# Memory's inputs in places of their own, both heads' sample scores in one bank, and three early products in a fused transformer step

## The chip, the core and the metric

The kernel runs on one core of a Trainium2 chip. The metric is the device time of one execution in microseconds (us). Before the change it is 1798.29 us, the median of three runs (1796.28 to 1800.38).

## The reference

One inference step of a streaming encoder layer, for a prompt of 1024 frames and a sample of 64 frames that share the weights; model width 1024, 16 heads of 64 (8 of kind A, 8 of kind B). All in float32.

```python
def mem_kv(mem, g_mem, w_mkv, g_mk):                 # mem (1, 256, 1024): the memory
    kv = rms_norm(mem, g_mem) @ w_mkv                # (256, 2048)
    k = rms_norm(kv[..., :D_MODEL].reshape(b, n, H_M, HEAD_DIM_M), g_mk)
    v = kv[..., D_MODEL:].reshape(b, n, H_M, HEAD_DIM_M)
    return k, v
...
# prompt: qa .. vb, logf = in_proj(rms_norm(xp), w_in, ...)
oa = chunk_band_attn_prompt(qa, ka, va, rel_bias)    # A: band of 8 chunks of 64
ob = forget_attn_prompt(qb, kb, vb, logf)            # B: causal, with a forget gate
xp = xp + concat([oa, ob]) @ w_o
xp = xp + mem_attend(rms_norm(xp), mk, mv, w_mq, g_mq, w_mo)
xp = xp + conv_ffn(rms_norm(xp), ...)
# sample: the same, with keys and values from caches (A: 512 rows, B: 1024 rows) ahead of its own 64
oa = chunk_band_attn_sample(qa, ka, va, cache_a_k, cache_a_v, rel_bias)
ob = forget_attn_sample(qb, kb, vb, logf, cache_b_k, cache_b_v, cache_b_logf)
xs = xs + concat([oa, ob]) @ w_o
```

## The kernel before

Every matmul of float32 data is made of three on TensorE (PE): a tensor is split into a rounded high part (a cast on ScalarE, ACT) and a low part (a subtraction on VectorE, DVE, or GpSimd, POOL), and high times high, low times high and high times low are added up in PSUM. The kernel is one long program in stages: input projection and prompt attention of eight pairs of heads; the tail of the last pair's attention; memory's keys and values; the sample's attention; the output projection w_o; memory attention; the feed-forward. A scheduler sets each engine's order from the order in which the code gives the work out, except for instructions in `tc.keep_in_program_order`. `weave(main, subs)` lays matmul pieces (`main`) between smaller jobs (`subs`).

The change lies between the tail of attention and the first products of w_o, 574 to 734 us of the span.

*Memory.* `load_mem` brings memory's frames (memT) in two halves into tiles `s` of the attention's own pool `wk`, and splits them with the gain into `mhi` and `mlo` (`gained`: ACT L256, DVE L257). `load_wm` brings the weights w_mkv in 16 loads of 512 KB into `mwraw`, two buffers; `split_wm` casts half a load to `mwhi` (ACT, L657) and subtracts `mwlo` (L658), by turns on POOL and DVE. `mem_piece` makes six matmuls (L668); four pieces make one of 16 units (column block n, half t of the 256 rows), 64 pieces and 384 matmuls in all. `mem_end` evicts a unit: for keys the norm's inverse root by `rsq` (two steps on ACT, three on DVE), for values a scaled copy. `mem_turn` transposes keys a unit later.

*Attention's tail.* The last pair's scores, sums and evictions come in four calls of `substeps()`. `otmp` (ACT, L552) and `mix` (DVE, L553) evict the attention's sum out of PSUM bank O; mix goes to DRAM (`mixd`). `LEFT` says how many memory pieces are woven into each of the four calls: 0, 0, 0, 15.

*Samples.* A `Sample` is a pair of heads of the 64 sample frames; the list has four of kind B first (1024 cached rows), then four of kind A (512). `prep` transposes q and k and splits them, and adds the gate on POOL (L750); `splitk` splits the cached keys of one head into `kchi` (ACT, L762) and `kclo` (DVE, L763); `splitv` the values into `vc` (ACT, L770; POOL, L771). `score(h)` makes one head's scores (L783; L784 for the sample's own 64 rows) with the q of both heads as weights, so that only 64 of the 128 rows of bank S are of use; a reduction on DVE adds the bias and finds the maximum (L786, L788) for those 64 rows. After the second head: the exponential on ACT (L796), the reciprocal, and the normalization on POOL (L798). `turn` transposes the probabilities (L810) and splits them into `pth` and `ptl` (L811, L812), `sum` multiplies by the values (L823) and adds up both parts in `st` (L830) and `su` (L831), `out` transposes into `smix` (L835, L837). In turn x of the loop, sample x is scored, sample x-1 is finished and sample x+1 prepared, with `PER[x]` memory pieces woven in: 4, 8, 9, 12, 6, 5, 6, 0, 0.

*Products.* When no memory piece is left, `open_left` closes memory's pool and opens in its place the weight stream (`raw`, `hi`, `lo`: L904, L905), the tiles `a` of the attention's result and their stage; `load_mix` and `split_mix` bring `mixd` in eight loads and split it (ACT L964, DVE L965), all eight in one turn of the loop (`MIXES`). A product is 24 matmuls of 384 columns (L922). Two products are made early, beside sample 7's end and behind it; `project` makes the rest in the order ORDER, and evicts each into x1d, the residual sum.

The split of memory's weights, and the pool that holds them:

```python
left = ExitStack()
mp = left.enter_context(tc.tile_pool(name="mp", bufs=1, side="left"))
...
def split_wm(n, y):
    raw = wraw[n, y // 2][:, 2 * (y % 2):2 * (y % 2) + 2]
    ...
    act.copy(hi, raw)
    (dve if y % 2 else pool).tensor_tensor(lo, raw, f32(hi), op=ALU.subtract)
```

Of the kernel before, what the change touches and what calls it, by code (L numbers as in the profile page):

```python
# [26 lines left out]
LEFT = (0, 0, 0, 15)  # L27
PER = (4, 8, 9, 12, 6, 5, 6, 0, 0)
STAGE, MIXES = 4, 8
# [12 lines left out]
def hybrid_step(ctx: ExitStack, tc: tile.TileContext, i: dict, o: dict):  # L42
# [590 lines left out]

    left = ExitStack()
    mp = left.enter_context(tc.tile_pool(name="mp", bufs=1, side="left"))
    kmd = dram.tile([4, 2, P, 256], F32, name="kmd")
    vmd = dram.tile([2, P, T], F32, name="vmd")
    mem = [mp.tile([P, KT, 256], F32R, name=f"m{n}") for n in ("hi", "lo")]
# [3 lines left out]
    def load_mem(z):  # L642
        raw = wk.tile([P, N], F32, name="s", bufs=4)[:, :1024].rearrange("p (k t) -> p k t", k=4)
        nc.sync.dma_start(raw, i["memT"][4 * z:4 * z + 4].rearrange("k p t -> p k t"))
        for k in range(4):
            gained(mem[0][:, 4 * z + k], mem[1][:, 4 * z + k], raw[:, k], gcol[:, 3, 4 * z + k:4 * z + k + 1])

    def load_wm(n, z):
        raw = mp.tile([P, 4, 256], F32, name="mwraw", bufs=2)
        nc.sync.dma_start(raw.rearrange("p k c -> p (k c)"), i["w_mkv"][n, z])  # L650
        wraw[n, z] = raw

    def split_wm(n, y):
# [3 lines left out]
        act.copy(hi, raw)  # L657
        (dve if y % 2 else pool).tensor_tensor(lo, raw, f32(hi), op=ALU.subtract)  # L658
# [15 lines left out]
    def mem_end(n, t):  # L674
        pj = mpj.pop((n, t))[:, :256]
        kv = mp.tile([P, 256], F32, name="kv", bufs=2)
# [3 lines left out]
        if n < 4:  # L680
# [4 lines left out]
            dve.tensor_scalar(ms, ms, emem[:, t:t + 1], None, op0=ALU.add)  # L685
            rsq(mp, ms, r, 1)
# [17 lines left out]
    class Sample:  # L704
# [31 lines left out]
        def prep(self):  # L736
# [7 lines left out]
            self.q = mq.tile([P, 2, S], F32R, name="sq_", bufs=2)  # L744
            self.kn = [mq.tile([P, 2, S], F32R, name=f"skn{x}", bufs=2) for x in range(2)]
            gained(self.q, self.q[64:], tq[:, 0:2, :S], gd[:, p // 4, 0:1], slice(64, P))
# [9 lines left out]
        def splitk(self, h):  # L756
            k = self.kraw.pop(0)
            for c in range(self.nc):
# [3 lines left out]
                act.copy(hi, raw)  # L762
                dve.tensor_tensor(lo, raw, f32(hi), op=ALU.subtract)  # L763
                self.kc[h, c] = hi, lo

        def splitv(self):
            for c in range(self.nc):
                raw = self.craw.pop(0)
                v = mq.tile([P, 4, 2, 2, 64], F32R, name="vc", bufs=3)
                act.copy(v[:, :, :, 0], raw)  # L770
                pool.tensor_tensor(v[:, :, :, 1], raw, f32(v[:, :, :, 0]), op=ALU.subtract)  # L771
                self.vc.append(v)

        def score(self, h):
            n = self.ctx
            b, q, r = self.s, self.q.rearrange("p h t -> p (h t)"), slice(h * S, h * S + S)
            if h == 0:
                self.mx = wk.tile([P, 2], F32, name="smx", bufs=2)
            sp = ps.tile([P, 2, 512], F32, name="S", bufs=1)
            sn = bank("tq").rearrange("p (a b) -> p a b", a=4)  # L780
            for m in range(2):
                for c in range(self.nc):
                    pe.matmul(sp[:, c], q, self.kc[h, c][m], start=m == 0, stop=m == 1)  # L783
                pe.matmul(sn[:, 0, :S], q, self.kn[m][:, h], start=m == 0, stop=m == 1)  # L784
            sf = sp.rearrange("p a b -> p (a b)")
            dve.tensor_tensor_reduce(out=b[r, :n], in0=sf[r, :n], in1=b[r, :n], scale=-1.0, scalar=BIG,  # L786
                                     op0=ALU.add, op1=ALU.min, accum_out=self.mx[r, 0:1])
            dve.tensor_tensor_reduce(out=b[r, n:n + S], in0=sn[r, 0, :S], in1=b[r, n:n + S], scale=-1.0, scalar=BIG,  # L788
                                     op0=ALU.add, op1=ALU.min, accum_out=self.mx[r, 1:2])
            if h == 0:  # L790
                return
# [3 lines left out]
            dve.tensor_tensor(m1, self.mx[:, 0:1], self.mx[:, 1:2], op=ALU.min)  # L795
            act.activation(b[:, :n], b[:, :n], ACT.Exp, bias=m1, scale=-1.0, accum_out=sm)  # L796
            dve.reciprocal(sm, sm)
# [72 lines left out]
    for n in LEFT:  # L870
        step(n, substeps())
# [978 lines left out]
```

## Time and profile before

| | |
|---|---|
| time, median of 3 runs | 1798.29 us (1796.28 to 1800.38) |
| the profiled execution's own time | 1797.27 us |
| its span, first to last instruction | 1795.2 us |
| mean granted clock of TensorE | 0.990 |
| busy share PE, DVE, ACT, POOL | 96%, 68%, 52%, 37% |
| memory's matmuls, first to last | 602.2 to 704.4 us |

The profile covers one execution. A timeline row gives the start, the duration, the engine, the line, the operation, output<-input, the shapes, how many rows are drawn together, and in brackets the idle time of the engine ahead of it with the event that ended it. PE overlaps its matmuls, so the distance of two starts says what one costs, and the duration does not. A group's row gives the count, then busy us and the mean ns of one, then the idle time of the engine ahead of the group and what ended it. The clock column is the share of full speed that TensorE was granted.

### The profile page before, as it was taken

How to read it: one execution, taken by the hardware profiler on the slowest of the kernel's cores; microseconds unless marked ns; L12 is line 12 of the kernel's file. 1: busy time of each engine (PE TensorE's matmuls, PEld its weight loads, DVE VectorE, ACT ScalarE, POOL GpSimd, SP SyncE). 2: the span in 40 equal slices, each digit the busy share in tenths (PEclk: the TensorE clock that was granted, in tenths of full speed). 3: DMA queues.
4: the chain of work that ended last, by engine and by line, in shares of the span. 5: the costliest groups of instructions: out<-in, count | busy, mean ns of one | idle time of the engine just before them, and what ended most of it. 6: DMA issues, size and time to landing. Idle time of an engine off the chain costs nothing. (4 is left out here: it accounts for less than half of the span.)

```text
span 1795.2 us, 34082 instructions
## 1 busy us (share of the span) xinstructions
PE 1716.4 (96%) x12432; PEld 1664.3 (93%) x12432; DVE 1224.5 (68%) x2710; ACT 930.2 (52%) x2042; POOL 664.1 (37%) x1025
## 2 busy tenths in 40 slices
PE   6898999999998888999999999999999999999999
PEld 5788999999997777999999999999999999999999
DVE  5778667677677797433444379877777777677994
ACT  5656667677677577433555455433333333434332
POOL 5656657779777554443444521100000000000000
PEclk8999999999999999999999999999999999999999
DMA  7322222122112776542111563222222222794232
GB/s 244 93 68 57 62 75 72 55 72 76 47 59 79 221 246 216 164 137 65 54 54 60 149 216 103 78 79 74 87 83 89 73 73 72 254 312 157 77 118 80
DMA packets 134248, 199.87 MB, mean 111 GB/s; under 512 B 20968, under 2 KB 74088, under 8 KB 134080
## 3 DMA queue, kind: packets, MB, share of 16 engines
q1 hardware_dynamic: 134080, 197.70, 34.8%
q8 instruction: 98, 1.61, 0.4%
q14 instruction: 70, 0.57, 0.1%
HBM read 155.35 MB, written 45.44 MB: 112 GB/s over the span
## 5 line engine op out<-in xcount | busy, mean ns | idle before, releaser
L288 PE MATMUL pj<-whi,xhi 128*128 128x384 f32 (+1 forms) x512 | 194.9, 381 | 3.4 <-ACT xhi L130 1.7
L288 PE MATMUL pj<-wlo,xhi 128*128 128x384 f32 (+1 forms) x512 | 176.1, 344 | 3.4 <-POOL wlo L123 3.4
L288 PE MATMUL pj<-whi,xlo 128*128 128x384 f32 (+1 forms) x512 | 174.7, 341 | 0.7 <-DVE xlo L131 0.7
L1540 POOL COPY s<-gp 128x2 f32<-128x2 f32 x22 | 15.8, 719 | 335.8 <-DVE gp L1539 335.8
L1434 PE MATMUL W<-h,hi 128*128 128x272 f32 x704 | 134.4, 288 | 1.4 <-ACT qlo L1570 1.4
L493 ACT ACTIVATE s<-s,mx 128x640 f32<-128x640 f32 (+7 forms) x128 | 94.4, 737 | 75.0 <-DVE mx L491 74.1
L1731 PE MATMUL W<-f,hi 128*128 128x272 f32 x672 | 127.7, 288 | 3.5 <-DVE f L1299 1.7
L530 DVE TENSOR_TENSOR ptl<-PT,pth 128x512 fp32r<-128x512 f32 (+2 forms) x192 | 99.5, 522 | 39.1 <-ACT pth L529 37.0
L1434 PEld LDWEIGHTS W<-h,hi 128*128 128x128 f32 x704 | 110.8, 188 | 1.7 <-ACT qlo L1570 1.6
L1731 PEld LDWEIGHTS W<-f,hi 128*128 128x128 f32 x672 | 105.3, 188 | 4.4 <-DVE gp L1505 2.4
L243 POOL TENSOR_TENSOR r<-m,mhalf 128x4 f32<-128x4 f32 (+1 forms) x72 | 73.9, 1027 | 92.4 <-DVE m L242 90.0
L529 ACT CAST pth<-PT 128x512 fp32r<-128x512 f32 (+2 forms) x192 | 85.0, 448 | 39.5 <-PE PT L528 37.9
L288 PEld LDWEIGHTS pj<-whi,xhi 128*128 128x128 f32 x512 | 98.9, 193 | 5.2 <-ACT xhi L130 2.3
L288 PEld LDWEIGHTS pj<-wlo,xhi 128*128 128x128 f32 x512 | 98.7, 193 | 5.3 <-POOL wlo L123 5.1
L1434 PE MATMUL W<-h,lo 128*128 128x272 f32 x352 | 101.8, 289 | 0.0
L1298 ACT CAST hi<-raw 128x512 fp32r<-128x512 f32 x68 | 42.2, 621 | 109.1 <-PE W L1434 59.1
L288 PEld LDWEIGHTS pj<-whi,xlo 128*128 128x128 f32 x512 | 97.3, 190 | 1.4 <-DVE xlo L131 1.2
L1731 PE MATMUL W<-f,lo 128*128 128x272 f32 x336 | 96.7, 288 | 0.0
L528 PE MATMUL PT<-ident,s 128*128 128x128 f32 x528 | 89.7, 277 | 6.2 <-DVE ptl L530 5.4
L246 POOL TENSOR_SCALAR qk<-qkraw,r 128x128 f32<-128x128 f32 x256 | 91.5, 375 | 5.9
L488 PE MATMUL S<-kh,q 128*128 128x256 f32 (+1 forms) x304 | 77.4, 280 | 12.8 <-DVE mx L491 12.7
L922 PE MATMUL pj<-a,hi 128*128 128x384 f32 (+1 forms) x352 | 89.5, 337 | 0.0
(606 smaller groups left out, 6051.3 us busy)
## 6 DMA issues: line engine op xcount, KB each, us to landing
raw<-in_w_down_dram SPq DMA_DIRECT2D x45, 256.0 KB, 2.9
wraw<-in_w_dram SPq DMA_DIRECT2D x56, 192.0 KB, 2.4
raw<-in_w_up_dram SPq DMA_DIRECT2D x41, 256.0 KB, 2.8
h<-ad SPq DMA_DIRECT2D x32, 272.0 KB, 4.7
mwraw<-in_w_mkv_dram SPq DMA_DIRECT2D x16, 512.0 KB, 5.2
raw<-in_w_mo_dram SPq DMA_DIRECT2D x32, 256.0 KB, 3.3
kvraw<-in_w_down_dram SPq DMA_DIRECT2D x32, 256.0 KB, 3.3
ad<-t SPq DMA_DIRECT2D x22, 272.0 KB, 2.1
```

The source lines that it names most:

```text
L243: pool.tensor_tensor(r[:rows], m[:rows], mhalf[:rows, 0:4], op=ALU.pow)
L246: pool.tensor_scalar(qk[:rows, h], raw[:rows, h * 64:(h + 1) * 64].rearrange("p (o d) -> p o d", o=1).broadcast_to([rows, 2, 64]), r[:rows ...
L288: pe.matmul(pj[:, :nw], x2[a][:, k, t * P:(t + 1) * P], wt[k][b][:, :nw], start=n == 0, stop=n == 3 * KT - 1)
L488: pe.matmul(sp[:, a:a + (k1 - k0) * P], q, kk[:, h, src], start=m == 0, stop=m == 1)
L493: act.activation(s[:, :n], s[:, :n], ACT.Exp, bias=mx, scale=-1.0, accum_out=sm)
L528: pe.transpose(pt[:, b - ch[0]], self.s[j][:, (b - w0) * P:(b - w0 + 1) * P], ident)
L529: act.copy(hi[:, f:f + n, j], pt[:, f:f + n])
L530: dve.tensor_tensor(lo[:, f:f + n, j], pt[:, f:f + n], f32(hi[:, f:f + n, j]), op=ALU.subtract)
L922: pe.matmul(out()[:, :cn], w[a][:, k % 4], x[b][k][:, c0:c0 + cn], start=k == 0 and n == 0, stop=k == KT - 1 and n == 2)
L1298: act.copy(hi, t)
L1434: pe.matmul(w[:, z, :Q], a(p, j), rights[j][b][:, z * Q:z * Q + Q], start=fresh and begin and j == 0 and x == 0, stop=final and end and j ...
L1731: pe.matmul(ws[m][:, z, :Q], la[p][:, m * P:(m + 1) * P], ra[b][:, z * Q:z * Q + Q], start=first and y == 0 and what in opening, stop=fina ...
```

## The change

1. *Memory's inputs.* memT gets tiles of its own (`mwraw`, now four buffers) and is loaded ahead of all else; its splits (`split_mem`, L651 and L652) are woven into attention's tail. All `mwlo` go to POOL. `rsq` in `mem_end` becomes an addition and a power on POOL (L691, L692). `kv` has three buffers, `mem_turn` comes two units later. Pools are opened with `reuse_waits="tile"`: a reused place waits for the tile that held it, not for the whole pool. ACT, DVE and POOL steps of these splits are kept in program order.
2. *Pieces.* LEFT becomes 0, 7, 7, 7, 6 (the first for the splits alone, the last beside the first sample's preparation), PER becomes 8, 8, 8, 7, 6, 0, 0, 0, 0.
3. *Samples.* `score` makes both heads at once: q lies in a tile with zeros (`zq`), so that each head's matmuls add zero to the other's 64 rows of one bank; the reductions run over 128 rows, once instead of twice. The normalization on POOL is gone; `sum` scales by the reciprocal instead (ACT and DVE).
4. *Products.* The stream's first weights are loaded while memory still runs. The splits of `mixd` come four in turn 6 and four in turn 7, the low parts by turns on DVE and POOL. Three products (0,0), (0,1), (1,0) are made early, in turns 7 and 8, stored in x1d, and read again in `project` at their places in a new ORDER. The sample's columns are split in one operation each on ACT and DVE.

```diff
-LEFT = (0, 0, 0, 15)
-PER = (4, 8, 9, 12, 6, 5, 6, 0, 0)
-STAGE, MIXES = 4, 8
+LEFT = (0, 7, 7, 7, 6)
+PER = (8, 8, 8, 7, 6, 0, 0, 0, 0)
+STAGE, MIXES = 4, {6: 4, 7: 4}
+EARLY = {7: (0,), 8: (1, 2)}
...
-    def load_mem(z):
-        raw = wk.tile([P, N], F32, name="s", bufs=4)[:, :1024].rearrange("p (k t) -> p k t", k=4)
-        nc.sync.dma_start(raw, i["memT"][4 * z:4 * z + 4].rearrange("k p t -> p k t"))
-        for k in range(4):
-            gained(mem[0][:, 4 * z + k], mem[1][:, 4 * z + k], raw[:, k], gcol[:, 3, 4 * z + k:4 * z + k + 1])
+    def split_mem(k):
+        raw, g = mraw[k // 4][:, k % 4], gcol[:, 3, k:k + 1]
+        keep(act.activation(mem[0][:, k], raw, ACT.Copy, scale=g))
+        keep(dve.scalar_tensor_tensor(mem[1][:, k], raw, g, f32(mem[0][:, k]), op0=ALU.mult, op1=ALU.subtract))
...
-        act.copy(hi, raw)
-        (dve if y % 2 else pool).tensor_tensor(lo, raw, f32(hi), op=ALU.subtract)
+        keep(act.copy(hi, raw))
+        keep(pool.tensor_tensor(lo, raw, f32(hi), op=ALU.subtract))
...
-            dve.tensor_scalar(ms, ms, emem[:, t:t + 1], None, op0=ALU.add)
-            rsq(mp, ms, r, 1)
+            pool.tensor_scalar(ms, ms, emem[:, t:t + 1], 1.0, op0=ALU.add, op1=ALU.mult)
+            pool.tensor_tensor(r, ms, mhalf[:, 0:1], op=ALU.pow)
...
-            for m in range(2):
-                for c in range(self.nc):
-                    pe.matmul(sp[:, c], q, self.kc[h, c][m], start=m == 0, stop=m == 1)
-                pe.matmul(sn[:, 0, :S], q, self.kn[m][:, h], start=m == 0, stop=m == 1)
+            for h in range(2):
+                q = self.z[:, 2 * h:2 * h + 2].rearrange("p h t -> p (h t)")
+                for m in range(2):
+                    first, last = h + m == 0, h + m == 2
+                    for c in range(self.nc):
+                        pe.matmul(sp[:, c], q, self.kc[h, c][m], start=first, stop=last)
+                    pe.matmul(sn[:, 0, :S], q, self.kn[m][:, h], start=first, stop=last)
...
-            pool.tensor_scalar(b[:, :n], b[:, :n], sm, 1.0, op0=ALU.mult, op1=ALU.mult)
...
-                    act.copy(t[r], self.op[r, h * P + 64:h * P + P])
-                    dve.tensor_tensor(self.u[r], self.op[r, h * P:h * P + 64], t[r], op=ALU.add)
+                    act.activation(t[r], self.op[r, h * P + 64:h * P + P], ACT.Copy, scale=self.r[r])
+                    dve.scalar_tensor_tensor(self.u[r], self.op[r, h * P:h * P + 64], self.r[r], t[r], op0=ALU.mult, op1=ALU.add)
...
-            act.copy(mixr[0][k][:, 0:T], raws[k])
-            dve.tensor_tensor(mixr[1][k][:, 0:T], raws[k], f32(mixr[0][k][:, 0:T]), op=ALU.subtract)
+            keep(act.copy(mixr[0][k][:, 0:T], raws[k]))
+            keep((pool if k % 2 else dve).tensor_tensor(mixr[1][k][:, 0:T], raws[k], f32(mixr[0][k][:, 0:T]), op=ALU.subtract))
...
+    EARLIEST = [(0, 0), (0, 1), (1, 0)]
+    ORDER = [(1, 1), (0, 2), (0, 0), (1, 2), (0, 1), (2, 0), (1, 0)] + [(m, c) for m in range(2, 8) for c in range(3)][1:]
...
+        subs = mix_splits[:MIXES.get(x, 0)] + subs if x in EARLY else subs + mix_splits[:MIXES.get(x, 0)]
+        del mix_splits[:MIXES.get(x, 0)]
+        for n in EARLY.get(x, ()):
+            main += early_product(n)
+        weave(main, subs) if main else place(subs, [])
```

Line numbers of the changed kernel lie one higher in attention (L552 is its L553) and some more behind: the splits of weights are its L663 and L664, memory's matmuls L674, the scores L792, the output's transpose L842, the products L929.

In the orders that follow a row is the line, the operation, output<-input, the shape, and how often it stands in a row. First ACT in attention's tail, where `vf` and `sq` belong to the last sample's projection. Before:

```order
L256 ACTIVATE q<-tq,gd 128x2x128
L256 ACTIVATE mhi<-s,gcol 128x256
L233 ACTIVATE sq<-sm 64x256
L344 ACTIVATE vf<-sm,rstd_81 64x128
L256 ACTIVATE mhi<-s,gcol 128x256 x3
L657 CAST mwhi<-mwraw 128x512 x2
L552 COPY otmp<-O 64x256
L529 CAST pth<-PT 128x4x128 x2
```

And with the change:

```order
L257 ACTIVATE q<-tq,gd 128x2x128
L234 ACTIVATE sq<-sm 64x256
L345 ACTIVATE vf<-sm,rstd_81 64x128
L553 COPY otmp<-O 64x256
L651 ACTIVATE mhi<-mwraw,gcol 128x256 x2
L494 ACTIVATE s,ssum<-s,mx 128x896
L530 CAST pth<-PT 128x4x128
L499 ACTIVATE s<-s,ssum 128x896
```

The eviction otmp now stands ahead of memory's splits, and the casts of weights have moved behind attention's next exponentials.

POOL from the end of attention's softmax to the first sample's gate (`stok`). Before:

```order
L496 TENSOR_SCALAR s<-s,ssum 128x1024
L658 TENSOR_TENSOR mwlo<-mwraw,mwhi 128x512
L496 TENSOR_SCALAR s<-s,ssum 128x1024
L750 TENSOR_SCALAR s<-s,stok 128x1088
L753 AFFINE_SELECT s<-s 64x64 x2
```

And with the change:

```order
L664 TENSOR_TENSOR mwlo<-mwraw,mwhi 128x512
L476 AFFINE_SELECT s<-s 128x128
L664 TENSOR_TENSOR mwlo<-mwraw,mwhi 128x512 x3
L497 TENSOR_SCALAR s<-s,ssum 128x1024
L691 TENSOR_SCALAR mms<-mms,emem 128x1
L692 TENSOR_TENSOR mr<-mms,mhalf 128x1
L664 TENSOR_TENSOR mwlo<-mwraw,mwhi 128x512 x4
L691 TENSOR_SCALAR mms<-mms,emem 128x1
L692 TENSOR_TENSOR mr<-mms,mhalf 128x1
L757 TENSOR_SCALAR s<-s,stok 128x1088
```

The gate of the first sample now stands behind more of memory's low parts, and behind the pairs mms and mr that were not on this engine.

PE at the last samples. Before, from the first scores of sample 7 back:

```order
L668 MATMUL pj<-mwhi,mhi 128x256
L668 MATMUL pj<-mwlo,mhi 128x256
L668 MATMUL pj<-mwhi,mlo 128x256
L743 MATMUL tq<-ident,sqd 128x64 x4
L835 MATMUL PT<-ident,su 64x128
L810 MATMUL PT<-ident,s 128x128 x2
L783 MATMUL S<-kchi,sq__10580 128x512
```

And with the change, from sample 7's preparation to the first product (the transposes of `s` are sample 6's):

```order
L749 MATMUL tq<-ident,sqd 128x64 x4
L817 MATMUL PT<-ident,s 128x128 x4
L817 MATMUL PT<-ident,s 64x128
L792 MATMUL S<-kchi,sq_9255 128x512
L793 MATMUL tq<-skn_10546,sq_9255 128x64
L793 MATMUL tq<-skn_10547,sq_9255 128x64
L793 MATMUL tq<-skn_10546,sq_9255 128x64
L793 MATMUL tq<-skn_10547,sq_9255 128x64
L792 MATMUL S<-kclo,sq_9255 128x512
L792 MATMUL S<-kchi,sq_9255 128x512
L792 MATMUL S<-kclo,sq_9255 128x512
L929 MATMUL pj<-ahi,hi 128x384 x2
```

Memory's matmuls no longer stand beside the last three samples, and the first product begins right behind sample 7's scores.

More of the change, by code (lines that the diff above doesn't have):

```diff
@@ L847, in piece @@
                 if n < 7:
-                    if t == 0 and c in (1, 2):
+                    if t == 0 and c in (1, 2) and n:
                         load_wm(n + 1, c - 1)
@@ L852, in piece @@
                 mem_piece(n, t, c)
-                if c == 2 and u:
-                    mem_turn(*units[u - 1])
+                if c == 1 and u > 1:
+                    mem_turn(*units[u - 2])
                 if c == 3:
@@ L857, in hybrid_step @@
             line.append(piece)
-    line.append(lambda: mem_turn(*units[-1]))
     def step(n, subs):
@@ L862, in step @@
         del line[:n]
-    load_wm(0, 0)
-    load_mem(0)
-    load_wm(0, 1)
-    load_mem(1)
-    split_wm(0, 0)
-    split_wm(0, 1)
-    for n in LEFT:
+    for z in range(2):
+        load_wm(0, z)
+    splits = [lambda k=k: split_mem(k) for k in range(KT)] + [lambda: split_wm(0, 0), lambda: split_wm(0, 1), lambda: load_wm(1, 0), lambda: load_wm(1, 1)]
+    weave(substeps(), splits)
+    for n in LEFT[1:-1]:
         step(n, substeps())
@@ L903, in upto @@
                 lo = self.pl.tile([P, 4, P], F32R, name="lo", bufs=4)
-                act.copy(hi, raw)
-                (dve if self.n >= 48 else pool).tensor_tensor(lo, raw, f32(hi), op=ALU.subtract)
+                two = act.copy(hi, raw), (dve if self.n >= 48 else pool).tensor_tensor(lo, raw, f32(hi), op=ALU.subtract)
+                if self.n < 4:
+                    for ins in two:
+                        keep(ins)
                 self.tiles[self.n] = hi, lo
```

157 lines of the change are left out of this document (79 added, 78 removed).

## The prediction

> **What bounds the kernel now.** I read the engine totals first, then the busy time in five stretches around the edit, then the timelines of TensorE (PE), ScalarE (ACT) and VectorE (DVE) where PE stands idle.
>
> ```profile
> span 1795.2 us, 34082 instructions
> PE 1716.4 (96%) x12432; PEld 1664.3 (93%) x12432; DVE 1224.5 (68%) x2710; ACT 930.2 (52%) x2042; POOL 664.1 (37%) x1025
> 574.00:602.00 28.00, 16.74 (x100) 13.78 (x99) 20.92 (x40) 20.58 (x41) 17.22 (x22) 0.82 0.75 233
> 626.00:704.00 78.00, 69.80 (x488) 60.18 (x487) 65.69 (x163) 52.74 (x134) 37.77 (x34) 1.00 0.75 240
> 704.00:730.00 26.00, 20.38 (x99) 17.45 (x98) 19.82 (x44) 18.11 (x44) 11.86 (x8) 0.80 0.51 170
> 730.00:800.00 70.00, 70.00 (x425) 70.00 (x424) 24.01 (x38) 26.82 (x52) 33.97 (x30) 1.00 0.51 158
> ```
>
> Behind the span come stretches: start and end, length, then PE, weight loads, DVE, ACT, POOL (GpSimd), granted clock, DMA share, GB/s. Over the program PE is the bound. Here it is not: from 574 to 602 it is busy 16.74 of 28 us, from 704 to 730 20.38 of 26 at a clock of 0.80, and in the 78 us between, DVE is busy 84% of the time. From 730 on PE never pauses. PE's order is the same in both kernels up to 573.79 us and from the fourth product on, and DVE (24.01) and ACT (26.82) have room in the 70 us behind. So the edit is worth what it moves the end of the third product. The next rows give that mark and those ahead of it.
>
> ```profile
> 573.79 1.06 PE L528 MATMUL PT<-ident,s 128*128 128x128 f32 x8
> 582.52 0.55 PE L543 MATMUL O<-pth,v 128*128 128x256 f32 x1 [7.67 <-DVE mix L553]
> 602.16 0.28 PE L668 MATMUL pj<-mwhi,mhi 128*128 128x256 f32 x1
> 602.28 0.28 PE L668 MATMUL pj<-mwlo,mhi 128*128 128x256 f32 x1
> 626.29 0.40 PE L783 MATMUL S<-kclo,sq__9225 128*128 128x512 f32 x1
> 691.27 0.48 PE L783 MATMUL S<-kclo,sq__10292 128*128 128x512 f32 x1
> 701.25 0.50 PE L783 MATMUL S<-kclo,sq__10437 128*128 128x512 f32 x1 [0.90 <-DVE kclo L763]
> 704.36 0.28 PE L668 MATMUL pj<-mwhi,mlo 128*128 128x256 f32 x1
> 705.94 0.50 PE L783 MATMUL S<-kchi,sq__10580 128*128 128x512 f32 x1
> 708.26 0.47 PE L783 MATMUL S<-kclo,sq__10580 128*128 128x512 f32 x1
> 713.47 0.42 PE L835 MATMUL PT<-ident,su 128*64 128x128 f32 x1 [3.36 <-DVE su L831]
> 714.58 1.01 PE L922 MATMUL pj<-a,hi 128*128 128x384 f32 x2
> 730.05 0.51 PE L922 MATMUL PT<-a,hi 128*128 128x384 f32 x2
> 730.40 0.34 PE L922 MATMUL PT<-a,lo 128*128 128x384 f32 x1
> 730.58 0.51 PE L922 MATMUL PT<-a,hi 128*128 128x384 f32 x2
> ```
>
> Memory's first matmul starts at 602.16 and one follows another by 0.12 us; the last of 384 ends at about 704.5. The first sample's scores end at 626.3 (132 memory matmuls are done by then), the last three samples' last scores stand at 691.27, 701.25 and 708.26. Three matmuls of the third product take 0.53 us from 730.05 to 730.58, so its 24 take 4.2 and it ends at 734.25: the mark to beat.
>
> **Attention's tail.** The 7.67 us hole is a queue that waits its turn:
>
> ```profile
> 577.84 1.14 ACT L657 CAST mwhi<-mwraw 128x512 fp32r<-128x512 f32 x2 [1.30 <-DMA mwraw<-in_w_mkv_dram]
> 579.00 0.37 ACT L552 COPY otmp<-O 64x256 f32<-64x256 f32 x1
> 579.00 2.92 DVE L658 TENSOR_TENSOR mwlo<-mwraw,mwhi 128x512 fp32r<-128x512 f32 x1 [1.96 <-ACT mwhi L657]
> 581.96 0.42 DVE L553 TENSOR_TENSOR mix<-O,otmp 64x256 f32<-64x256 f32 x1
> 579.60:584.60 5.00, 1.71 (x6) 1.45 (x7) 4.97 (x7) 4.62 (x10) 3.71 (x4) 0.50 0.51 146
> 712.80:717.80 5.00, 2.94 (x10) 2.19 (x11) 3.62 (x5) 4.71 (x9) 3.13 (x2) 0.50 0.91 289
> 717.80:722.90 5.10, 5.10 (x19) 4.95 (x19) 5.07 (x7) 4.64 (x12) 2.72 (x3) 0.50 0.75 280
> ```
>
> On ACT otmp stood behind mhi and two weight casts that waited for their DMA; on DVE mix stood behind one mwlo of 2.92 us. Both idle stretches of PE (7.67 and 3.36 us) are followed by some 10 us at clock 0.50. The new order puts otmp ahead of every memory operation, and no weight split is left on DVE, so this hole and its half clock go: 7.7 us, and some 2 us of half clock (an estimate: PE was busy 1.71 of five of those ten us, more in the other five), with no price but the later start of the splits. With LEFT, memory's matmuls then stand among attention's last ones, from about 586 on.
>
> What is late next is POOL, which now makes every mwlo and memory's mr. Its groups between 574 and 730 (count, busy us, mean ns, idle time ahead and releasers; L243's is over the whole program):
>
> ```profile
> L658 POOL TENSOR_TENSOR mwlo<-mwraw,mwhi 128x512 fp32r<-128x512 f32 x16 | 22.7, 1424 | 8.2 <-ACT mwhi L657 4.4 <-ACT rsq_y L77 2.9 <-DMA svn<-sv 0.8
> L771 POOL TENSOR_TENSOR vc<-vraw,vc 128x512 fp32r<-128x512 f32 x12 | 15.5, 1291 | 25.1 <-ACT vc L770 25.1
> L905 POOL TENSOR_TENSOR lo<-raw,hi 128x512 fp32r<-128x512 f32 x4 | 8.3, 2096 | 5.0 <-DMA mraw<-mixd 2.6 <-ACT hi L904 2.4
> L243 POOL TENSOR_TENSOR r<-m,mhalf 128x4 f32<-128x4 f32 (+1 forms) x72 | 73.9, 1027 | 92.4 <-DVE m L242 90.0
> L246 POOL TENSOR_SCALAR qk<-sm,r 64x128 f32<-64x128 f32 x4 | 1.4, 365 | 0.1
> L750 POOL TENSOR_SCALAR s<-s,stok 128x1088 f32<-128x1088 f32 x4 | 5.1, 1286 | 3.9 <-PE PT L528 2.7 <-DMA s<-negs 1.3
> ```
>
> From the first split to the first sample's mask POOL's new order holds 16 mwlo (22.7 us), 7 pairs of mms and mr (the pow has L243's form, 1.03, and the scalar step at most L246's 0.37: 9.8) and some 3 us of softmax and mask: 36 us, and some 4 of waiting. From 587 that is 627 for the first sample's scores, where they were. But 180 memory matmuls stand ahead of them, not 132: 48 x 0.12 = 5.7 us that are won, and the rest of the 15 us by which memory starts earlier is given back here.
>
> **The samples with memory.** Behind that mark 204 memory matmuls are left, beside samples 0 to 4 (before, 252 beside 0 to 6). DVE's groups between 626 and 704:
>
> ```profile
> L658 DVE TENSOR_TENSOR mwlo<-mwraw,mwhi 128x512 fp32r<-128x512 f32 x10 | 9.6, 963 | 0.9 <-ACT mwhi L657 0.8
> L786 DVE CUSTOM_DVE_ANT_0 s<-S,s 64x1024 f32<-64x1024 f32 x7 | 8.5, 1220 | 0.4 <-PE S L783 0.2
> L786 DVE CUSTOM_DVE_ANT_0 s<-S,s 64x512 f32<-64x512 f32 x6 | 4.1, 686 | 0.8 <-PE S L783 0.4
> L763 DVE TENSOR_TENSOR kclo<-kraw,kchi 128x512 fp32r<-128x512 f32 x18 | 18.2, 1027 | 1.1 <-ACT kchi L762 1.1
> L812 DVE TENSOR_TENSOR ptl<-PT,pth 128x512 fp32r<-128x512 f32 x10 | 6.8, 677 | 0.0
> ```
>
> Of DVE's 65.69 us in the 78 there leave it: the splits 9.6, and half of the score reductions, 6.3 (a reduction over 128 rows costs what one over 64 does, since time goes by elements in a row: 1024 take 1220 ns, 512 take 686); the removed steps of rsq are a few us more. At the old pace the 204 matmuls would end at about 690 (54.4 us from the first sample's last scores to sample 4's, and 9 for what is left). The floor is PE: 204 x 0.12 = 24.5, and the samples' own share: 69.8 less 252 x 0.12 = 39.6 for a little over six of them, 26 for four: 50.5, so 677.5. DVE no longer sets the pace, POOL nearly does; I take the end of memory at 682, with 677 and 690 as ends. The score matmuls are as many as before (both heads into one bank by zero-padded q); dropping the POOL normalization (L798, about 1 us) shortens each sample's chain, and the scaling in the sums costs nothing new.
>
> **The end.** From 704.5 to 730.05 the old kernel needs 25.6 us for sample 7 without memory beside it, the mix splits and two products. The new one has samples 5 and 6 without memory as well. A bare sample: 7.0 us by the step from 701.25 to 708.26 (few memory matmuls in it); at most 8.6 (sample 7's from its first scores at 705.94 to the product behind its transposes at 714.58, the 3.36 us wait within), and at least 5.7 (10.0 us between 691.27 and 701.25, less 36 memory matmuls). Two of them: 14.0. Then 25.6 again (the mix loads are early now, but half of the low parts move to POOL), and 4.2 for the third product. The group that splits them, between 574 and 730:
>
> ```profile
> L965 DVE TENSOR_TENSOR a<-mraw,a 128x1024 fp32r<-128x1024 f32 x8 | 11.1, 1393 | 1.8 <-ACT a L964 1.6
> ```
>
> Four stay on DVE (5.6 us); four on POOL cost twice a 128x512 row there, 2.6 each by vc or 4.2 by lo, so 10 to 17 us, behind lo (8.3) and vc in the queue. I take 2.6, since of vc there are more. They lie beside sample 7 unless the queue slips. The order has x1 stored and read again for the three early products: DMAs beside PE's 70 us without a pause; the last columns' splits become one operation on each engine where there were eight, at the same place; mem_turn stands two units later with one more kv buffer: I cost all three at nothing.
>
> Sum: 682 + 14.0 + 25.6 + 4.2 = 725.8 against 734.25: 8.4 us won. The profiled execution took 1797.27 (span 1795.2 and 2.1 around it), 1.0 below the median of 1798.29; the forecast for the median is 1790.
>
> [...]
>
> **Rivals.** *Full gain.* Memory ends at PE's floor (677), bare samples take 5.7, and no PE pause of 3 us comes, so that the half clock of 712.8 to 722.9 and its some 5 us are gone: 677 + 11.4 + 20.6 + 4.2 = 713, 21 us won, 1777. For it: the mix loads and weights are there early. Against it: bare samples have nothing to fill PE.
>
> *POOL's queue sets the pace: slower.* In program order each vc on POOL waits for its ACT half (25.1 us of idle time between 574 and 730), and now all mwlo stand behind it; before, every other one went by DVE. If mwlo takes 1.75 us, half way to lo, the first 16 put the first scores at 632. Behind them POOL has 16 more (28), ten vc (13), masks and svh (some 6) and half of that waiting (12): 59 us, memory ends at 691. With bare samples of 8.6 and one alo of 4 us that PE waits for: 691 + 17.2 + 29.8 + 4 = 742, 8 us lost, 1806. It decides from the point where memory ends later than 690. For it: 22.7 us of mwlo become 45. Against it: POOL is busy only 37.77 of 78 us.
>
> *Given back.* Memory at 687 and bare samples of 8.6: 687 + 17.2 + 29.8 = 734, no change, 1798. Nothing beside samples 5 and 6 is exactly what the earlier memory buys.
>
> **Numbers.** Forecast (4 to 16 us won) 0.50, full gain 0.16, given back (within 0.2%, 3.6 us, which is about what a measurement tells from no change) 0.17, slower 0.17. Low 1777 is full gain, high 1803 half way into the slower rival. The forecast's own range is 1783 to 1795.
>
> **What would show it.** Right: no hole at 574.9 and the first L674 (L668 before) near 587; the first sample's scores at 627 behind 180 memory matmuls; the last memory matmul at 677 to 690; DVE below 75% beside samples 0 to 4; third product's end 726. Wrong: mwlo or alo as what PE waits for, POOL near 90% before 682, clock 0.50 beside samples 5 or 6, or a time moved behind 735.

## The result, and the profile after

The changed kernel takes 1820.42 us (median of four runs, 1819.94 to 1823.72) against 1798.52 before: a ratio of 1.0125, with a 95% interval of 1.0113 to 1.0137 (before was run once more with it, so its median is 0.2 above the one forecast from). It is 22 us slower, and the forecast was 8 us faster, with 1803 as the high end.

First the page's totals and the busy time by stretch, of the changed kernel; the columns are those of the rows of before.

```profile
span 1818.8 us, 33972 instructions
PE 1732.8 (95%) x12432; PEld 1677.7 (92%) x12432; DVE 1188.9 (65%) x2619; ACT 927.7 (51%) x2019; POOL 689.1 (38%) x1055
574.00:602.00 28.00, 21.50 (x157) 20.18 (x155) 15.04 (x33) 19.16 (x41) 20.28 (x24) 0.88 0.71 214
626.00:704.00 78.00, 69.01 (x429) 60.94 (x429) 37.29 (x94) 46.20 (x108) 40.19 (x41) 0.87 0.64 191
704.00:730.00 26.00, 15.33 (x51) 10.54 (x51) 13.91 (x32) 14.63 (x33) 8.22 (x7) 0.56 0.68 213
730.00:800.00 70.00, 65.04 (x358) 61.30 (x359) 26.04 (x41) 26.40 (x54) 35.42 (x27) 0.92 0.47 145
```

DVE fell from 65.69 to 37.29 us in the 78. That is more than the 16 us and a few of the prediction's sum, in part because one sample fewer is scored in the stretch. POOL did not rise much. Yet no engine is near full between 704 and 730: PE is busy 15.33 of 26 us, at a clock of 0.56. The stretch waits. Now PE's marks, in the same form as before:

```profile
584.37 0.31 PE L674 MATMUL pj<-mwhi,mhi 128*128 128x256 f32 x1
630.63 0.49 PE L792 MATMUL S<-kclo,sq 128*128 128x512 f32 x1
698.63 0.28 PE L674 MATMUL pj<-mwhi,mlo 128*128 128x256 f32 x1
702.62 0.40 PE L792 MATMUL S<-kclo,sq 128*128 128x512 f32 x1
719.40 0.80 PE L792 MATMUL S<-kclo,sq 128*128 128x512 f32 x1 [0.46 <-DVE kclo L770]
727.01 0.63 PE L792 MATMUL S<-kclo,sq 128*128 128x512 f32 x1
755.75 0.33 PE L929 MATMUL pj<-ahi,lo 128*128 128x384 f32 x1
```

These are memory's first matmul (18 us earlier than before), the first sample's last scores, memory's last matmul, the last scores of samples 5, 6 and 7, and the end of the third product: 755.9, where 734.25 was the mark to beat. The 21.7 us between the two are nearly all of the 23.6 by which the two profiled spans differ (1818.8 and 1795.2), so the loss lies in these stretches, as the prediction had placed its gain. Against the prediction's terms the first scores are 3.6 us late, memory's end 16.7 us (698.7 for 682), and the rest takes 57.2 us for 43.8.

What stands in the way beside sample 1 is POOL's queue, and DVE behind it; timelines of the changed kernel:

```profile
634.99 1.28 POOL L664 TENSOR_TENSOR mwlo<-mwraw,mwhi 128x512 fp32r<-128x512 f32 x1 [1.53 <-ACT mwhi L663]
636.23 2.51 POOL L778 TENSOR_TENSOR vc<-vraw,vc 128x512 fp32r<-128x512 f32 x2
638.69 3.73 POOL L664 TENSOR_TENSOR mwlo<-mwraw,mwhi 128x512 fp32r<-128x512 f32 x3
642.75 0.55 POOL L692 TENSOR_TENSOR mr<-mms,mhalf 128x1 f32<-128x1 f32 x1
640.01 0.58 PE L674 MATMUL pj<-mwlo,mhi 128*128 128x256 f32 x1 [2.72 <-POOL mwlo L664]
643.34 0.48 DVE L693 SCALAR_TENSOR_TENSOR kv<-pj,mr,gmk 128x256 f32<-128x256 f32 x1 [5.70 <-POOL mr L692]
```

POOL all but never stops from 635 to 643. PE waits 2.72 us for an mwlo behind two vc, and DVE's kv waits 5.70 for an mr behind three mwlo, with the next sample's kclo behind it.

### The profile page after: what moved, and what is told of

It is laid out like the page before. It is cut to its first block, busy times and chain, and to the rows that moved or that the text cites. A ratio compares the mean times of both kernels' runs of the same rounds, so it can differ in the third digit from the quotient of the medians.

```text
span 1818.8 us, 33972 instructions
## 1 busy us (share of the span) xinstructions
PE 1732.8 (95%) x12432; PEld 1677.7 (92%) x12432; DVE 1188.9 (65%) x2619; ACT 927.7 (51%) x2019; POOL 689.1 (38%) x1055
## 4 chain that ended last, share of the span: by engine, by line
PE 44%; DVE 5%; DMA 2%; issue 1%; POOL 1%; ACT 0%; SPq 0%; POOLq 0%; ACTq 0%; DVEq 0%
PE W L1445 25%; PE pj L929 7%; PE W L1742 7%; PE W L929 2%; DMA raw<-in_w_down_dram 1%; PE S L1188 1%; DVE lo L1310 1%; PE tq L1224 1%; PE O L1224 1%; POOL lo L909 1%; DVE f L1310 1%; PE PT L1211 0%; DVE h L1677 0%; DVE f L1516 0%; PE O L1188 0%
## 5 line engine op out<-in xcount | busy, mean ns | idle before, releaser
L497 POOL TENSOR_SCALAR s<-s,ssum 128x640 f32<-128x640 f32 (+6 forms) x96 | 68.3, 713 | 35.9 <-DVE ssum L495 30.6
```

Of the source, the lines that this page charges most:

```text
L497: pool.tensor_scalar(s[:, :n], s[:, :n], sm, 1.0, op0=ALU.mult, op1=ALU.mult)
```

## The experiments

Times are medians; "less" is against the changed kernel's 1820.4, unless another is named. The numbers in brackets are the ratio to the kernel before and its 95% interval.

**Parts undone, one at a time.** lo_turns:

```diff
-        keep(pool.tensor_tensor(lo, raw, f32(hi), op=ALU.subtract))
+        keep((dve if y % 2 else pool).tensor_tensor(lo, raw, f32(hi), op=ALU.subtract))
```

> One part undone: memory's mwlo by turns on POOL and DVE again, as before the change. Theory POOL (its queue paces memory: PE waits 0.6 to 2.7 us at a time for mwlo beside samples 0 to 4, and these pauses bring the half clock): PE's waits for POOL mwlo between 626 and 700 (some 7 us) mostly go, memory ends 8 to 12 us earlier than at 698.7, total 1808 to 1813. Theory CLOCK (the loss lies in the samples without memory, at half clock from 708 to 737): memory's end moves by 0 to 4 us, total 1816 to 1821. Theory MR (DVE waits for mr, which stands behind mwlo and vc on POOL): the queue ahead of mr is halved, 4 to 6 us, total 1814 to 1817.

Measured 1812.93, 7.5 us less (ratio to before 1.0082, interval 1.0067 to 1.0097). Memory's end moves from 698.7 to 693.4, the first scores from 630.6 to 625.1. PE's wait for mwlo, changed kernel and then lo_turns, between 574 and 756:

```profile
L674 PE MATMUL pj<-mwlo,mhi 128*128 128x256 f32 x128 | 41.1, 321 | 10.5 <-POOL mwlo L664 10.4
L674 PE MATMUL pj<-mwlo,mhi 128*128 128x256 f32 x128 | 39.4, 308 | 7.4 <-POOL mwlo L664 6.6 <-DVE mwlo L664 0.8
```

The total lies in theory POOL's range, but its mechanism held only in part. The wait falls by only 3.1 us, and memory's end moves by 5.3 where the theory had 8 to 12, so most of the 7.5 comes some other way (read in the timeline, not tried: what else stands behind the mwlo in POOL's queue). Of the 7.5, 5.5 are there already at the first scores. This is about a third of the loss, and the samples without memory are late all the same.

mr_back, the inverse root on ACT and DVE again:

```diff
-            pool.tensor_scalar(ms, ms, emem[:, t:t + 1], 1.0, op0=ALU.add, op1=ALU.mult)
-            pool.tensor_tensor(r, ms, mhalf[:, 0:1], op=ALU.pow)
+            dve.tensor_scalar(ms, ms, emem[:, t:t + 1], None, op0=ALU.add)
+            rsq(mp, ms, r, 1)
```

> One part undone: the inverse root of memory's keys by ACT and DVE again (rsq) in place of the power on POOL. Theory MR: kv on DVE no longer waits for POOL (5.70 us at 643.34, 3.21 at 620.95, 2.57 at 628.89), kclo behind it comes earlier; 8 us less, 1811 to 1815. Theory POOL: POOL's queue is 16 short operations (0.26 and 0.56 us each) shorter, under 7 us of 120: 0 to 3 us less, 1817 to 1821. Theory CLOCK: the half clock of 637 to 647 goes with the pause, that of 708 to 737 stays: 3 to 5 us less, 1815 to 1818.

1821.60, no gain (1.0131, 1.0109 to 1.0152). The 5.70 us wait is real and covered: from 574 to 756 kv waits 24.9 us for mr in the changed kernel and nothing here, and the time stays. Theory MR falls.

alo_dve (`alo` is the low part of the mix, `ahi` its high part):

```diff
-            keep((pool if k % 2 else dve).tensor_tensor(mixr[1][k][:, 0:T], ...))
+            keep(dve.tensor_tensor(mixr[1][k][:, 0:T], ...))
```

> One part undone: all eight low parts of the mix on DVE (before: all on DVE; in the change four on POOL). Theory POOL, in the tail: PE's waits for alo (0.85 at 730, 1.64 at 747) and for vc behind them (1.54 at 733.6) go, with the half clock that they prolong: 4 to 7 us less, 1813 to 1816. Theory CLOCK: the pauses of 1.3 to 2 us between 703 and 725 come ahead of any alo, so the half clock stays: 0 to 3 us less, 1817 to 1821.

1816.14, 4.3 us less (1.0097, 1.0082 to 1.0112), the upper end of theory POOL's range. The wait is that of vc in the queue between alo; POOL and then PE and DVE of the changed kernel:

```profile
727.30 2.73 POOL L973 TENSOR_TENSOR alo<-mraw,ahi 128x1024 fp32r<-128x1024 f32 x1 [5.65 <-ACT ahi L972]
730.00 2.33 POOL L909 TENSOR_TENSOR lo<-raw,hi 128x512 fp32r<-128x512 f32 x1
732.28 1.26 POOL L778 TENSOR_TENSOR vc<-vraw,vc 128x512 fp32r<-128x512 f32 x1
733.50 3.35 POOL L973 TENSOR_TENSOR alo<-mraw,ahi 128x1024 fp32r<-128x1024 f32 x1
733.60 0.58 PE L830 MATMUL O<-vc,pth 128*128 128x256 f32 x1 [1.54 <-POOL vc L778]
732.44 2.18 DVE L973 TENSOR_TENSOR alo<-mraw,ahi 128x1024 fp32r<-128x1024 f32 x1 [1.18 <-ACT ahi L972]
```

spread, memory's pieces beside samples 0 to 6 (here the third early product's residual is loaded over the first's before that is added, which leaves the work the same):

```diff
-PER = (8, 8, 8, 7, 6, 0, 0, 0, 0)
-STAGE, MIXES = 4, {6: 4, 7: 4}
-EARLY = {7: (0,), 8: (1, 2)}
+PER = (5, 5, 6, 6, 5, 5, 5, 0, 0)
+STAGE, MIXES = 4, {7: 8}
+EARLY = {8: (0, 1, 2)}
```

> Memory's last 37 pieces spread over samples 0 to 6 (5, 5, 6, 6, 5, 5, 5) instead of 0 to 4 (8, 8, 8, 7, 6); for that the mix splits lie all in turn 7 and the three early products in turn 8. Theory CLOCK: samples 5 and 6 have matmuls beside them, the half clock of 29 us from 708 is cut to the 10 that the kernel before has; 10 to 15 us less, 1805 to 1811. Theory POOL: the waits for mwlo are only laid elsewhere, and the mix splits come later: 0 to 5 us less, 1815 to 1821. If the early products pay for themselves only beside the mixes' earlier splits, it is slower than 1821.

1814.26, 6 us less (1.0083, 1.0066 to 1.0099), between the two theories: sample 7's last scores come 8.8 us earlier, at 718.2 for 727.0, but part of it is lost again behind them, where all mix splits now lie in one turn.

**Is it the clock?** fill adds matmuls that nobody needs beside samples 5 and 6:

```diff
+        for _ in range(2):
+            pe.matmul(pf[0][:, :256], zero[:, :P], zero, start=True, stop=True)
...
+        if x in (5, 6):
+            main = [fill] * 24
```

> The changed kernel with 96 added matmuls (128x256, zeros, into a PSUM bank that nobody reads) beside samples 5 and 6, where memory's pieces are gone; 11.5 us of work at full clock. They change no result. Theory CLOCK: PE pauses there no longer, the half clock from 708 to 737 goes, and the stretch gets 6 to 12 us shorter although there is more to do: 1808 to 1815. Theory CHAIN (each step there waits for ACT, DVE and POOL, and the clock is only a mark of it): the added matmuls fill the pauses or stand in the way, 1819 to 1828.

1819.13, within the noise of the changed kernel (1.0122, 1.0107 to 1.0137). The stretch in the changed kernel and then in fill:

```profile
700.00:720.00 20.00, 12.27 (x47) 8.12 (x47) 9.70 (x23) 9.52 (x25) 6.05 (x5) 0.68 0.78 232
700.00:720.00 20.00, 19.59 (x144) 17.76 (x144) 10.10 (x28) 9.99 (x24) 5.00 (x5) 1.00 0.81 255
```

PE is busy 19.59 of 20 us at full clock, and sample 7's last scores still come at 725.5 (727.0). In the bare samples (those without memory beside them) the half clock is a mark of the waiting, not its cause: there theory CLOCK falls.

**Is it memory at all?** hihi leaves out two of memory's three products:

```diff
-        for m in range(6 * c, 6 * c + 6):
+        for m in range(6 * c, 6 * c + 6, 3):
```

> The changed kernel without two of memory's three products (low times high, high times low): 128 of its 384 matmuls are left, so PE waits for no mwlo and has 30.5 us less to do there at full clock; POOL still makes every mwlo. The memory's keys and values are those of the high parts. Theory PIECES (memory's matmuls, or their wait for mwlo, set when the first early products can begin): 20 us less or more, 1792 to 1802. Theory SAMPLES (the chain of samples, each through ACT, DVE and POOL, sets it, and memory only fills): 2 to 8 us less, 1812 to 1818.

1817.26, 3 us less (1.0111, 1.0095 to 1.0127), although 256 matmuls are gone:

```profile
626.00:704.00 78.00, 57.72 (x275) 44.82 (x275) 38.17 (x93) 47.07 (x108) 41.67 (x40) 0.76 0.75 227
```

This is the run that matters most for the prediction. PE waits instead, at a lower clock. Memory's last matmul comes 13 us earlier, at 685.6, and 30 us of work less (256 at 0.12) bring sample 7's last scores only 5.5 us forward (721.5). In the changed kernel memory's matmuls are mostly filling, and an early end of them is worth little in itself. (POOL still makes every mwlo here, so this says nothing of that work.)

**The loads.** In the changed kernel the first four mix loads stand ahead of sample 6's on SP; SP's timeline:

```profile
700.78 1.89 SPq L969 DMA_DIRECT2D mraw<-mixd  x4
702.76 0.57 SPq L722 DMA_DIRECT2D sqd<-sqk  x1
705.40 1.01 SPq L735 DMA_DIRECT2D kraw<-in_cak_dram  x2
```

loads_first issues the sample's first (`open_left()` behind `nxt.load()`).

> The changed kernel with one thing turned round on SP: sample 6's loads are issued ahead of the first four mix loads (2 MB), which stand ahead of them in the change. Theory LOADS (sample 6 comes 17 us after sample 5 because its q, values and keys wait behind the mix loads): its first operations at 712 to 714 come 5 to 8 us earlier, total 1812 to 1816. Theory CHAIN (the bare samples wait for one another's steps on ACT, DVE and POOL): 0 to 2 us, 1818 to 1821.

1817.27, 3.1 us less (1.0103, 1.0090 to 1.0117), between the two theories: sample 6's scores end 8.8 us earlier, at 710.6, and sample 7's 5 us, at 722.0, so more than half is lost again behind.

one_load loads the caches once; for keys (the values' loads are changed in the same way):

```diff
+                if len(caches) < 2:
+                    raw = mq.tile([P, T], F32, name="kraw", bufs=2)
+                    nc.sync.dma_start(raw, self.ck[2 * (p % 4) + h])
+                    caches.append(raw)
+                self.kraw.append(caches[h][:, :self.ctx])
```

> The changed kernel, in which the cached keys and values are loaded once, for the first sample, and all eight samples work on these tiles (so the outputs of the other seven pairs of heads are those of the first's caches); every engine operation is left. Theory LOADS (SP's queue and the transfers set the samples' pace, since SP waits 14.5 us for kclo and 9.4 for vc before it can issue the next loads): 96 us from sample 0's scores to sample 7's become 80 or less, total 1800 to 1808. Theory STEPS (the engines' queues set it: POOL's mwlo and mr, DVE behind kv, ACT behind vc): 0 to 5 us less, 1815 to 1820.

1804.21, 16.2 us less (1.0027, 1.0017 to 1.0036): theory LOADS. Sample 0 to sample 7 takes 83.4 us instead of 96.4, a little more than the 80 that the theory had. The run takes away the waits in SP's queue and the transfers alike (the DMA share of 626 to 704 falls from 0.64 to 0.48), and does not tell the two apart. What SP waits for in the changed kernel between 600 and 722 (us in total, times, longest):

```profile
SPq L735 <- DVE kclo L770: 14.5, 4, 6.5
SPq L694 <- DVE kv L693: 12.7, 4, 4.9
SPq L697 <- ACT kv L696: 11.3, 3, 5.3
SPq L739 <- POOL vc L778: 9.4, 3, 4.3
```

L735 and L739 are the loads of cached keys and values, which wait for a buffer; L694 and L697 are memory's stores, which wait for their data with the loads behind them in the one queue.

**Together.** lo_alo_loads has lo_turns, alo_dve and loads_first in one.

> mwlo by turns, alo on DVE and sample 6's loads ahead of the mix loads, memory's pieces as in the change (samples 5 and 6 bare). Of lo_turns and alo_dve alone the sum would be 1808.6. Theory LOADS: 1800 to 1804, near lo_alo_six (1798.7), whose pieces beside sample 5 are then only a way to lay the mix loads a sample later. Theory BARE (samples without memory beside them are dear in themselves): 1807 to 1809.

1804.30 (1.0030, 1.0018 to 1.0043). That is 0.3 above theory LOADS' range and below theory BARE's. The three single gains add up to 14.9 us, which gives 1805.5; the expectation had counted two of them.

lo_alo_six has lo_turns and alo_dve, and spreads the pieces as `PER = (6, 6, 7, 6, 6, 6, 0, 0, 0)`:

> The changed kernel with mwlo by turns on POOL and DVE, alo all on DVE, and memory's last 37 pieces over samples 0 to 5 (6, 6, 7, 6, 6, 6), so that one sample is bare ahead of sample 7 instead of two; mix splits and early products stay in turns 6, 7 and 8. If the three gains add up (7.5 of lo_turns, 4.3 of alo_dve and half of the spread's 6): 1803 to 1808. Theory CLOCK: more, since the last pauses of PE go with it, 1796 to 1802.

1798.69, the time of before (1.0003, 0.9993 to 1.0012). With memory ending a sample later (698.5) the kernel is 10 us faster than the sum of lo_turns and alo_dve. That is theory CLOCK's range. But fill speaks against the clock as a cause, and the order of loads alone gives 4.3 of the 10 (lo_alo_loads against the same sum); what gives the rest is not shown.

> lo_alo_six (1798.7; pieces over samples 0 to 5, mwlo by turns, alo on DVE) with sample 7's loads ahead of the first four mix loads. If the order of loads and the spreading of the pieces are one cause, nothing more: 1797 to 1800. If they are two, 3 us more as in loads_first: 1794 to 1797.

1801.26 (1.0014, 1.0004 to 1.0023), 2.6 us above lo_alo_six: neither expectation. The edit is that of loads_first on lo_alo_six. The two gains don't add; with the pieces spread, the order of loads is no gain, and why it costs something is open.

lo_spread_alo spreads further, with the pieces and splits of spread, and the third early product's residual loaded behind the first's end:

> As lo_alo_six, but with the pieces over samples 0 to 6 (5, 5, 6, 6, 5, 5, 5), all eight mix splits in turn 7 and the three early products in turn 8, in sequence (the third's residual is loaded behind the first's end). What is left of the change is the head (otmp first, memory from 587 on), the one bank and the third early product. If the gains add up: 1820.4 - 7.5 - 4.3 - 6 = 1803. If the head is worth its hole of 7.7 us and nothing else is lost: 1790 to 1796, below the kernel before.

1801.70 (1.0018, 1.0009 to 1.0028): near the 1803 of the first case, in which the gains add up, and outside the 1790 to 1796 of the second, in which the head is worth its hole.

**One part alone, on the kernel before.** bank_alone takes `score`, `sum` and the zero-padded q from the change, and nothing else:

> The kernel before with one part of the change alone: both heads' scores in one bank (zero-padded q, one reduction for both), the normalization in the sums. By the prediction's sum this takes some 6 us off DVE in the stretch where DVE is busy 84%, and a step of about 1 us off each sample's chain: 1789 to 1796. Theory CHAIN: both heads' key splits are now needed before any score is complete, while before the second head's splits lay beside the first head's reduction; each sample gets later by a microsecond or two: 1797 to 1806.

1793.20, faster than both kernels: 0.9975 (0.9965 to 0.9984), about 4.5 us, inside the expected 1789 to 1796.

bank_head adds the head: tiles of its own for memT, `split_mem` woven into attention's tail, `LEFT = (0, 7, 7, 7, 6)`, `PER = (5, 5, 6, 6, 5, 5, 6, 0, 0)`.

> bank_alone (the kernel before with both heads' scores in one bank, 1793.2) with the change's head: memT in tiles of its own, otmp ahead of memory's splits, memory's pieces among attention's last ones and then 5 or 6 beside samples 0 to 6; mwlo by turns, rsq, mix splits and two early products as before. By the prediction's sum, closing the 7.7 us hole and starting memory 15 us earlier is worth 5 to 10 us: 1783 to 1788. Theory SAMPLES: the samples start where they did, and memory only fills beside them: 1791 to 1796.

1797.36 (0.9996, 0.9987 to 1.0005), 4 us above bank_alone and above both theories' ranges: with the one bank, the head costs time. bank_hole closes the hole alone:

```diff
-    split_wm(0, 0)
-    split_wm(0, 1)
-    for n in LEFT:
+    weave(substeps(), splits + [lambda: split_wm(0, 0), lambda: split_wm(0, 1)])
+    for n in LEFT[1:]:
```

> bank_alone (1793.2) with one thing more: memory's first splits are given out within attention's last scores instead of ahead of them, so that otmp and mix stand ahead of most of them and the 7.7 us hole can close; pieces (LEFT, PER), tiles and loads are as before. Theory HOLE (the hole is worth its length and its half clock): 1783 to 1788. Theory SAMPLES (the first sample's scores come when its gate and keys are there, at 627, whatever attention's tail does): 1791 to 1795. bank_head lost 4 us: if the hole is the gain and the early pieces the loss, this kernel is 5 to 10 us below bank_head (1797.4).

1794.73 (0.9973, 0.9964 to 0.9983), in theory SAMPLES' range. bank_alone and then bank_hole, by stretch:

```profile
574.00:602.00 28.00, 16.96 (x101) 14.23 (x102) 21.25 (x40) 19.82 (x39) 18.18 (x23) 0.82 0.75 236
626.00:704.00 78.00, 74.57 (x514) 64.45 (x512) 55.77 (x144) 57.17 (x144) 33.09 (x28) 0.98 0.73 235
574.00:602.00 28.00, 20.23 (x118) 17.83 (x119) 20.41 (x40) 19.92 (x39) 16.68 (x22) 0.76 0.73 241
626.00:704.00 78.00, 68.99 (x476) 59.83 (x476) 58.39 (x138) 53.95 (x132) 32.15 (x30) 1.00 0.69 226
```

The hole is closed: PE is busy 3.3 us longer in the tail, and the first scores come 3.7 us earlier (624.0 for 627.7). But PE is busy 5.6 us less in the samples, and sample 7's last scores come at 707.2 where they came at 706.2. The idle time has changed its place.

> bank_alone (1793.2) with the cached keys and values loaded once for all samples (the outputs of seven pairs of heads are then those of the first's caches). Theory LOADS (they set the samples' pace there too): 1780 to 1787. Theory PE (in this kernel, where PE is busy 74.57 of the 78 us from 626 to 704, the matmuls set it): 1790 to 1794.

This is one_load's edit on bank_alone. 1792.52 (0.9970, 0.9959 to 0.9981), not told from bank_alone: the loads set nothing here. The same edit on bank_hole:

> bank_hole (1794.7) with the caches loaded once. Against bank_one_load it tells what hides the closed hole. If the loads hide it: 3 to 8 us below bank_one_load. If something else does (the mix loads, sample 7's chain, the two products): within 2 us of bank_one_load.

1795.94 (0.9983, 0.9974 to 0.9992), 3.4 above bank_one_load with intervals that overlap. Neither theory had it there, but it is not below, so it isn't the loads that hide the closed hole.

bank_deep is bank_alone with four buffers of `kraw` and `vraw`, and `STAGE` 3:

> bank_alone with four buffers instead of three for the cached keys and values (and three instead of four for the mix). Theory LOADS in its narrow form (SP waits for a free key or value buffer and holds back all loads behind): 2 to 5 us less than 1793.2. If the transfers themselves are the matter, 1792 to 1795.

1793.74 (0.9974, 0.9963 to 0.9985), the same: the narrow form of theory LOADS falls here. None of bank_alone's variants is told from it as faster. What holds them near 1793 is open: neither loads, nor their buffers, nor the hole.

## Why the prediction was wrong, point by point

- *Which stretch.* Right: nearly the whole difference is the shift of the third product's end, 21.7 us of the 23.6 between the profiled spans.
- *Attention's tail.* otmp went ahead, the hole of 7.7 us went, memory began at 584.4, and 180 memory matmuls stood ahead of the first scores, all as said. But the hole was not clear gain: between 560 and 602 PE now waits 6.0 us for DVE's mx, where it had waited 0.8, and the clock is 0.50 from 577.6 to 584.4. The longest of these waits:

```profile
580.36 0.58 PE L489 MATMUL S<-kh,q 128*128 128x256 f32 x1 [3.47 <-DVE mx L492]
```

  The first scores came at 630.6 for 627. The worth of 5.7 us was wrong too: hihi shows that matmuls won in advance buy little (3 us for 256 of them), and bank_hole that the closed hole buys nothing that can be told.
- *Memory at 682.* This term failed first: it measured 698.7. It was worked out from PE's and DVE's work, as if the bound were the sum of an engine's durations. DVE was relieved by more than forecast, to 48%, and the time grew. What counts, as the timelines read, is what each sample waits for in turn: the samples' steps stand in the queues of POOL, DVE, ACT and SP, behind memory's. Of this hihi shows that PE's work is not the bound, and lo_turns puts the share of mwlo on POOL at 7.5 us.
- *Two bare samples, 14.0.* From sample 5's last scores to sample 7's took 24.4 us (16.8 and 7.6). The 7.0 of the row fitted the second and missed the first: in the kernel before, no sample was left to load when the mix loads came. "The mix loads are early now" was counted as a gain; the queue that they were moved past was SP's, with sample 6's loads behind them. loads_first gives back 3.1 us and moves sample 6 by 8.8.
- *The low parts on POOL beside sample 7, for nothing.* They cost 4.3 us (alo_dve). The size of one was right: 2.70 us each on POOL by the changed kernel's group, 2.6 forecast. Their cover was not there, since vc stood behind them: from sample 7's last scores to the third product's end took 28.9 us, where it had taken 26.0. The range's upper end, 1795, allows 5 us for this move: an estimate of the author's that no run shows by itself. Measured is the whole move, 4.3. How much of it is the queue, and how much that operations of DVE and POOL side by side took longer (last section), was not tried.
- *The one bank.* Right in kind: alone it gains 4.5 us. The prediction had 6.3 us of DVE's work and some 1 us of each sample's chain for it, and no time of its own. Its count of the reductions held: one over 128x1024 took 1225 ns in the changed kernel, where one over 64x1024 had taken 1220.
- *The rivals.* The slower one named the right queue and the wrong amount: 742 for the third product's end, measured 755.9. Its price for mwlo was wrong as well: the 32 took 1.31 us each and not 1.75, so the queue is late by what stands in it and waits, not by slower operations. It lacked the loads. Its point of decision, memory later than 690, held.

The loss, as far as runs divide it: mwlo on POOL 7.5, alo on POOL 4.3, and some 10 from where memory's pieces lie, and with them the mix loads (lo_alo_six against the sum of the first two): 21.7, back to the time before. The order of loads alone is 3.1 of it. Against bank_alone the changed kernel is 27 us slower. The 5.5 that lo_alo_six still has of this lie in parts that were not tried alone (the third early product, the pools' waits by tile, the program order kept for splits) and in the head, which cost bank_head 4.

Shown is that the loads hold the changed kernel's samples (one_load, 16.2 us) and that the same loads don't hold bank_alone's (0.7). That SP's waits for vc and kclo are the link, rather than the transfers, is read from the profile and was not tried alone. These 16.2 are not a loss beside the 21.7 but overlap with it: in lo_turns, without a change to the loads, SP's waits for kclo and kv fall from 14.5 and 12.7 us to 10.0 and 6.2 (that for vc is 11.1 for 9.4).

## What to carry to other kernels

An engine's busy share says what it could give back, not what the stage waits for (here DVE fell from 65.69 to 37.29 of 78 us, and the kernel took 22 us more): before an advance of one strand of work is counted, leave that work out in an experiment, as in hihi. Work moved to a less busy engine is not free when that engine's queue serves a chain in order (7.5 us for mwlo here, 4.3 for alo); list what stands behind each moved instruction, on the queue that issues loads too. Of a change in many parts, try the parts alone: one of these four was worth 4.5 us, and the others together took some 27.

## What the runs showed of the hardware

The half clock came here without a long pause of PE. In the changed kernel the clock is 0.50 throughout 708 to 738, while PE's longest pause from 700 to 738 is 1.97 us:

```profile
705.65 0.27 PE L842 MATMUL PT<-ident,su 128*64 128x128 f32 x1 [1.97 <-DVE su L838]
720.00:740.00 20.00, 15.04 (x52) 11.73 (x52) 11.01 (x21) 11.33 (x20) 10.72 (x7) 0.55 0.54 189
```

The full-gain rival had the half clock go where no PE pause of 3 us comes. That was the author's estimate (before, the half clock stood behind pauses of 7.67 and 3.36 us), and these rows are against it. With fill's dense matmuls (PE busy 19.59 us of 20) the clock was 1.00 from 700 to 720.

Where a subtraction on DVE and one on POOL overlapped in this stretch, the later one took longer. DVE's alo at 732.44 takes 2.18 us, where two others, which began when POOL was idle or about to end, took 1.21 each; POOL's vc runs until 733.5, and from there to DVE's end is 1.1. POOL's alo at 733.50 takes 3.35, where another, which began while DVE was idle, took 2.35:

```profile
729.97 1.21 DVE L973 TENSOR_TENSOR alo<-mraw,ahi 128x1024 fp32r<-128x1024 f32 x1
744.62 2.35 POOL L973 TENSOR_TENSOR alo<-mraw,ahi 128x1024 fp32r<-128x1024 f32 x1 [2.48 <-ACT ahi L972]
```

So the two took 0.97 and 1.00 us longer, about the 1.1 us that were left of the other engine's operation when each began. What makes them longer was not tried.
